# First high halves of the up-projection in one VectorE step, an early split of its third weight chunk, and the last results by TensorE halves and GpSimd

## The chip, the cores and the metric

The kernel runs on one core of one Trainium2 chip. The metric is the device time of one execution in microseconds (us), the median of several runs; lower is better.

## The reference

One layer of a decoder for 256 tokens of width 2048, in float32. Three parts follow one another, each with a norm ahead of it and a norm on its result before the result is added to the residual stream:

```python
x = x + rms_norm(hybrid_mixer(rms_norm(x, mix_pre_norm), ...), mix_post_norm)
h = rms_norm(x, xattn_pre_norm); m = rms_norm(mem, mem_norm)
x = x + rms_norm(cross_attention(h, m, ...), xattn_post_norm)
h = rms_norm(x, ffn_pre_norm)
x = x + rms_norm(conv_glu_ffn(h, w_up, conv_w, conv_b, w_down), ffn_post_norm)
...
def rms_norm(x, g):
    return x * lax.rsqrt(jnp.mean(x * x, axis=-1, keepdims=True) + 1e-6) * g
def conv_glu_ffn(h, w_up, conv_w, conv_b, w_down):
    u = h @ w_up                      # 2048 -> 16384
    uc = conv_b + sum(conv_w[j] * shift_right(u, 2 - j) for j in range(3))
    gate, up = split_cols(uc, (8192, 8192))
    return (jax.nn.gelu(gate, approximate=True) * up) @ w_down   # 8192 -> 2048
```

The change touches two places: the seam between cross-attention and the feed-forward part (the second and third `x = x + ...`), and the last residual addition, which is the output.

## The kernel before

**Three products for one.** Every large matrix product is made in the fast float32r format with compensation. A float32 operand is split into a high half (its rounding to float32r) and a low half (the rest), and TensorE adds up high times high, high times low and low times high. So each weight chunk and each activation tile has a high and a low half: `wh` and `wl` of the weights, and for the up-projection `fh` and `fl` of the normed residual (`hi` and `lo` in the code of `Residual`). ScalarE makes `wh` (L376), VectorE subtracts and gets `wl` (L397).

**Blocks and chunks.** The work is a list of blocks of 256 or 512 output columns, run in a fixed order by `run`. A block's weights come in chunks of 128x1024 (512 KB), each good for two of the 16 contraction tiles k of the up-projection. `Feed` loads the chunks in order through SP's DMA queue into four `raw` buffers; a buffer is free again when its `wl` has been made. `wh` and `wl` have four buffers each too. `feed.hi(n)` and `feed.lo(n)` split all chunks up to number n that are not split yet, in order; `ns` and `nl` count how far that is. The first two blocks of the up-projection (`entry`) are interleaved chunk by chunk, since the tiles of the activation come slowly at first: block 0 chunk 0, block 1 chunk 0, block 0 chunk 1 and so on. With four groups of columns, two tiles and three products, a chunk is 24 matmuls.

**Engines.** Program order on each engine is the order in which the Python code issues. Work beside the matmuls (evacuations, statistics, residuals) is written as generators, of which `run` takes a piece at each `side.half()`, by a budget of VectorE and ScalarE time.

**The seam.** The last block of the output projection of cross-attention (`xo3`) is computed bank by bank, so that the sum of squares for the norm of its result is nearly done when its last columns come. `y_last` has the three parts of that: `after` (once the first bank is done), `mid`, and `gen` at the end. TensorE sums the squares over the partitions (`stb`) and ScalarE makes 1/rms out of it in two steps, `st_b` (called `rb` in `Residual`). `Residual.run` then updates the residual x (`xr`) with the scaled result (`z`): for the first pair of tiles, tile by tile, `z *= rb` and `x += z` on VectorE, then `parts(0)`: `fh = x * g` on ScalarE (float32r) and `fl = x * g - fh` on VectorE, where g is the norm's gain (`pcol("fg", j)`). The factor of the norm itself is applied later, on the products. Later pairs are done two tiles at a time. Only from `fh` of tile 0 on can TensorE begin with the up-projection; until then it runs a few matmuls of no use (`warm`). For the first tile, the order is four times `fh` with `wh`, four times `fh` with `wl`, four times `fl` with `wh`; from the second tile on, `fh` with `wh`, `fl` with `wh`, `fh` with `wl` for each group of columns.

**The end.** `fd_evac` finishes the down-projection: for each half of the tokens (t) and four column groups c of 512, `out = x + z3 * rco`, where `z3` is the product times the gain and `rco` the 1/rms column. For t = 0 all of it runs beside the last matmuls. For t = 1 (`result(1, c)`) it can't. There column group 0 is made by TensorE (identity times x, then a diagonal matrix of `rco` times `z3`, added in PSUM as `sum`) and copied out by ScalarE, which also issues its DMA; groups 1 to 3 are made by VectorE one after the other, and SP issues their DMAs in order.

Of the kernel before, what the change touches and what calls it, by code (L numbers as in the profile page):

```python
# [11 lines left out]
AF = mybir.ActivationFunctionType  # L12
ALU = mybir.AluOpType
AX = mybir.AxisListType

P = 128
D = 2048
S = 256
# [127 lines left out]
def _layer(ctx, tc, nc, d, dbg):  # L146
    act, dve = Meter(nc.scalar, 200.0, 0.83), Meter(nc.vector, 70.0, 1.04)
# [11 lines left out]
    def T2(name, shape=None, dt=F32):  # L159
        return mp.tile(shape or [P, 2, S], dt, tag="T2", bufs=6, name=name)  # L160
# [16 lines left out]
    def aux(name, shape=None):  # L177
        return pp.tile(shape or [P, 512], F32, tag="aux", bufs=4, name=name)

    def mm(out, lhsT, rhs, start=True, stop=True):  # L180
        pe.matmul(out, lhsT, rhs, start=start, stop=stop, skip_group_check=True)  # L181
# [15 lines left out]
    def pcol(n, i=0, w=1):  # L197
        return par[:, PC[n] + i:PC[n] + i + w]
# [131 lines left out]
    class Feed:  # L330
# [49 lines left out]
        def first(self):  # L380
# [8 lines left out]
            self.st[0] = [wh, wl]  # L389
            self.ns = self.nl = 1  # L390

        def lo(self, upto):
            self.hi(upto)
            while self.nl <= min(upto, len(self.src) - 1):
                r = self.raw.pop(self.nl)
                wl = self.staged("wl", r, self.nl)
                nc.vector.tensor_sub(wl, r, self.st[self.nl][0])  # L397
                self.st[self.nl][1] = wl
                self.nl += 1
# [33 lines left out]
    def run():  # L433
# [8 lines left out]
        for b, c0, c1 in order:  # L442
# [23 lines left out]
            for ci, s in enumerate(srcs):  # L466
                if b["pre"]:
                    b["pre"](ci, feed)
                feed.lo(i + 1)
                side.half()  # L470
                side.more = lambda: feed.hi(i + 2)
                ahead = b["xs"](k)
                feed.lo(i + 3)
                feed.dma(i + 6)
                wh, wl = feed.st.pop(i)
                for kj in range(s.shape[1]):
                    xh, xl = b["xs"](k) if kj else ahead
                    first, last = k == 0, k == nk - 1
                    if b["kind"] == "fm":
                        steps = []  # L480
                        for m in range(nm):
                            o = banks[m // 2][:, m % 2]
                            a, c = wh[:, kj, m * P:(m + 1) * P], wl[:, kj, m * P:(m + 1) * P]
                            steps.append([(o, a, xh, first and m % 2 == 0, False), (o, c, xh, False, last),
                                          (o, a, xl, False, False)])
                        if first and entry and b is entry[0]:
                            steps = [[v[0] for v in steps], [v[1] for v in steps], [v[2] for v in steps]]
                        elif b is blocks[0] and k < 4:
                            steps = [[v[0] for v in steps], [v[2] for v in steps], [v[1] for v in steps]]
                        else:  # L490
                            steps = [[v[0], v[2], v[1]] for v in steps]
                        for v in steps:
                            for w in v:
                                mm(*w)
                    elif b is xv:
                        for g in range(2):
                            halves(banks, (wh[:, kj], wl[:, kj], xh, xl), first, last, g)
                    else:
                        for g, o in enumerate(banks):
                            n = o.shape[1]  # L500
                            tm_products(o, g * P * n // b["cols"], g * n % b["cols"], (wh[:, kj], wl[:, kj], xh, xl),
                                        first, last)
                            if len(banks) == 4 and g == 1:
                                side.half()
                    k += 1
                    if kj + 1 < s.shape[1]:
                        side.half()
                i += 1
# [868 lines left out]
    def y_last(b, st, key, gname):  # L1377
        def carry(src, m):
            act.activation(M[key][b // 2][:, (b % 2) * 4 + m], src, AF.Copy, scale=pcol(gname, b * 4 + m))

        def after(ps):
            st.add(ps[0])
            st.fold()

        def mid(ps):
            M["sql"] = C("sql", "bg0", [P, 2, S])
            act.activation(M["sql"][:, 0], ps[1][:, 0], AF.Square)
            for j in range(2):
                carry(ps[0][:, j], j)
            st.ones_of((st.acc[:, 0], M["sql"][:, 0]), start=True)  # L1390

        def gen(ps):
            end = xo3["apart"]
            act.activation(M["sql"][:, 1], end, AF.Square)
            st.ones_of((M["sql"][:, 1],), stop=True)
            carry(ps[1][:, 0], 2)
            st.last()
            yield
            carry(end, 3)
            yield  # L1400
        return after, mid, gen
# [4 lines left out]
    class Residual:  # L1406
# [8 lines left out]
        def run(self):  # L1415
            st, key, hi, lo, gname = self.a
            z, xr = M[key], M["xr"]
            for _ in range(10):
                if st.done:
                    break  # L1420
                yield
            while not st.done:
                side._piece(side.bulk[0])
            if self.early:
                rb = st.row()
            else:
                rb = st.rb
                keep_warm(5)

            def parts(i, js=(0, 1)):  # L1430
                for j in js:
                    k = i * 2 + j
                    act.activation(hi[:, k], part(xr, i)[:, j], AF.Identity, scale=pcol(gname, k))
                for j in js:
                    k = i * 2 + j
                    dve.scalar_tensor_tensor(lo[:, k], part(xr, i)[:, j], pcol(gname, k), hi[:, k],
                                             op0=ALU.mult, op1=ALU.subtract)
                self.ready = i + 1

            def scale(i):  # L1440
                dve.tensor_mul(part(z, i), part(z, i), bc(rb, 2))

            def add(i):
                dve.tensor_add(part(xr, i), part(xr, i), part(z, i))

            if self.early:
                yield
            a, x = part(z, 0), part(xr, 0)
            for j in range(2):
                dve.tensor_mul(a[:, j], a[:, j], rb)  # L1450
                dve.tensor_add(x[:, j], x[:, j], a[:, j])
            if self.early:
                scale(1)
                parts(0)
            else:
                parts(0)
                scale(1)
            yield
            for i in range(1, 8):
                if i == 1:  # L1460
                    add(1)
                if i < 7:
                    scale(i + 1)
                    add(i + 1)
                parts(i)
                if i == 1 and not self.early:
                    side.more()
                if self.early:
                    self.st2.add(part(xr, i - 1))
                    if i == 7:  # L1470
                        self.st2.add(part(xr, 7))
                        self.stats = side.add(self.st2.early_column(), chain=1, free=True)
                elif i == 6:
                    self.stats = side.add(self.squares(), chain=1)
                yield
# [332 lines left out]
    def load_gain():  # L1808
        M["gain"] = mp.tile([P, D], F32, tag="hT", bufs=2, name="gain")
        sp.dma_start(M["gain"], d["fpg"].partition_broadcast(P))  # L1810

    def fd_evac(n):

        def gen(ps):
# [28 lines left out]
            def result(t, c):  # L1843
                f = slice(c % 2 * 512, c % 2 * 512 + 512)
                x, z_ = M["xt"][c // 2][:, t, f], M["z3", c // 2][:, t, f]
                if t and c == 0:
                    diag = C("diag", "ysb0", [P, P])
                    act.activation(diag, ident, AF.Copy, scale=rco[:, t:t + 1])
                    mm(M["sum"], diag, z_, start=False)
                    act.copy(x, M["sum"])  # L1850
                else:
                    dve.scalar_tensor_tensor(x, z_, rco[:, t:t + 1], x, op0=ALU.mult, op1=ALU.add)
                (act if t and c == 0 else sp).dma_start(d["out"][t, :, c * 512:c * 512 + 512], x)
# [17 lines left out]
            result(0, 2)  # L1871
            result(0, 3)
            before_last(1)
            M["sum"] = aux("sum")
            mm(M["sum"], ident, M["xt"][0][:, 1, 0:512], stop=False)
            squares(3)
            finish(1)
            gain(3)
# [101 lines left out]
```

## Time and profile before

| | |
|---|---|
| time, median of 3 runs | 1876.56 us (1876.15 to 1876.88) |
| the profiled execution | 1877.65 us, its span 1875.6 us |
| TensorE (PE) busy | 1865.9 us, 99% of the span |
| VectorE (DVE) busy | 1293.7 us, 69% |
| ScalarE (ACT) busy | 1014.1 us, 54% |
| GpSimd (POOL) busy | 22.3 us, 1% |
| granted TensorE clock | 0.999 of full speed |

The span is what the profiler saw of the device's work; the time of the same execution is 2.05 us longer, and 1.09 us over the median. Times inside the span are counted from its start. In a row of the timeline the first number is the start, the second the duration (of all instructions of the row, if several were merged, "x2"), then engine, line, operation, output<-inputs and shape, and in brackets the idle time of the engine ahead of it with what ended it. In a row of the chain of waits there are start, duration, engine, tile and line. Instructions of one engine overlap a little at their ends, so the next may start before the last has ended. L66 and L181 are helpers through which most instructions go.

### The profile page before, as it was taken

How to read it: one execution, taken by the hardware profiler on the slowest of the kernel's cores; microseconds unless marked ns; L12 is line 12 of the kernel's file. 1: busy time of each engine (PE TensorE's matmuls, PEld its weight loads, DVE VectorE, ACT ScalarE, POOL GpSimd, SP SyncE). 2: the span in 40 equal slices, each digit the busy share in tenths (PEclk: the TensorE clock that was granted, in tenths of full speed). 3: DMA queues.
4: the chain of work that ended last, by engine and by line, in shares of the span. 5: the costliest groups of instructions: out<-in, count | busy, mean ns of one | idle time of the engine just before them, and what ended most of it. 6: DMA issues, size and time to landing. Idle time of an engine off the chain costs nothing.

```text
span 1875.6 us, 36356 instructions
## 1 busy us (share of the span) xinstructions
PE 1865.9 (99%) x15024; PEld 1777.8 (95%) x15024; DVE 1293.7 (69%) x1832; ACT 1014.1 (54%) x1477; POOL 22.3 (1%) x40
## 2 busy tenths in 40 slices
PE   9999999999999999999999999999999999999998
PEld 9999988999999999999999999999999988888887
DVE  7789787566675857687766666777666675566555
ACT  6776445555454645665554445554444555445554
POOL 0000000000000000000000000000000000000000
PEclk9999999999999999999999999999999999999999
DMA  7545544344455765455666666666666666666664
GB/s 266 184 166 195 180 150 161 129 148 157 169 181 204 279 201 183 143 182 167 202 190 192 196 198 192 194 190 192 200 195 194 196 192 215 193 192 196 193 191 145
DMA packets 98197, 351.46 MB, mean 187 GB/s; under 512 B 11056, under 2 KB 11568, under 8 KB 97648
## 3 DMA queue, kind: packets, MB, share of 16 engines
q1 hardware_dynamic: 97168, 348.01, 57.9%
q8 instruction: 117, 1.92, 0.4%
q10 hardware_dynamic: 864, 1.15, 0.2%
q14 instruction: 48, 0.39, 0.1%
HBM read 347.01 MB, written 2.10 MB: 186 GB/s over the span
## 4 chain that ended last, share of the span: by engine, by line
PE 97%; DVE 1%; ACT 1%; DMA 0%; issue 0%; ACTq 0%; DVEq 0%
PE fm L181 67%; PE tm L181 25%; DVE wl L397 1%; PE gram L181 0%; ACT wh L376 0%; PE Y L181 0%; PE lv L181 0%; PE num L181 0%; DMA w<-in_w_in_dram 0%; DVE rows L66 0%; PE X L181 0%; PE gramA L181 0%; PE U L181 0%; PE zg L181 0%; PE zwa L181 0%
## 5 line engine op out<-in xcount | busy, mean ns | idle before, releaser
L397 DVE TENSOR_TENSOR wl<-raw,wh 128x1024 fp32r<-128x1024 f32 (+1 forms) x640 | 776.0, 1217 | 418.5 <-ACT wh L376 415.6
L376 ACT CAST wh<-raw 128x1024 fp32r<-128x1024 f32 (+1 forms) x640 | 664.5, 1043 | 499.9 <-PE fm L181 373.2
L181 PE MATMUL fm<-fh,wh 128*128 128x256 f32 x2048 | 566.4, 277 | 1.4 <-ACT fh L66 1.4
L181 PE MATMUL fm<-fh,wl 128*128 128x256 f32 x2048 | 565.5, 276 | 0.0
L181 PE MATMUL fm<-fl,wh 128*128 128x256 f32 x2048 | 565.4, 276 | 0.0
L181 PEld LDWEIGHTS fm<-fh,wh 128*128 128x128 f32 x2048 | 384.3, 188 | 1.5 <-ACT fh L66 1.5
L181 PEld LDWEIGHTS fm<-fh,wl 128*128 128x128 f32 x2048 | 384.7, 188 | 0.1
L181 PEld LDWEIGHTS fm<-fl,wh 128*128 128x128 f32 x2048 | 384.3, 188 | 0.0
L181 PE MATMUL tm<-wh,as 128*128 128x512 f32 x1024 | 315.3, 389 | 0.0
L181 PE MATMUL fm<-hh,wh 128*128 128x256 f32 x1024 | 285.2, 281 | 0.2
L181 PE MATMUL fm<-hh,wl 128*128 128x256 f32 x1024 | 282.4, 278 | 0.7 <-DVE wl L397 0.7
L181 PE MATMUL fm<-hl,wh 128*128 128x256 f32 x1024 | 282.2, 278 | 0.0
L181 PEld LDWEIGHTS tm<-wh,as 128*128 128x128 f32 x1024 | 192.1, 188 | 40.0
L181 PE MATMUL tm<-wl,as 128*128 128x512 f32 x512 | 199.2, 389 | 0.0
L181 PEld LDWEIGHTS fm<-hh,wh 128*128 128x128 f32 x1024 | 192.4, 189 | 1.8 <-issue 0.3
L181 PEld LDWEIGHTS fm<-hh,wl 128*128 128x128 f32 x1024 | 191.4, 188 | 1.1 <-DVE wl L397 1.1
L181 PEld LDWEIGHTS fm<-hl,wh 128*128 128x128 f32 x1024 | 191.9, 188 | 0.1
L181 PEld LDWEIGHTS tm<-wl,as 128*128 128x128 f32 x512 | 96.1, 188 | 19.9
L66 ACT CAST as<-ac 128x256 fp32r<-128x256 f32 x128 | 45.6, 404 | 110.8 <-PE tm L181 110.8
L66 DVE TENSOR_TENSOR as<-ac,as 128x256 fp32r<-128x256 f32 x128 | 48.5, 421 | 61.7 <-ACT as L66 61.7
L181 PE MATMUL fm<-mgh,wh 128*128 128x256 f32 x256 | 71.0, 277 | 0.0
L181 PE MATMUL fm<-mgh,wl 128*128 128x256 f32 x256 | 70.8, 277 | 0.0
(383 smaller groups left out, 2220.3 us busy)
## 6 DMA issues: line engine op xcount, KB each, us to landing
raw<-in_w_fu_dram SPq DMA_DIRECT2D x256, 512.0 KB, 4.2
raw<-in_w_in_dram SPq DMA_DIRECT2D x152, 512.0 KB, 3.6
raw<-in_w_fd_dram SPq DMA_DIRECT2D x128, 512.0 KB, 3.9
raw<-in_w_br_dram SPq DMA_DIRECT2D x32, 512.0 KB, 3.8
raw<-in_w_mo_dram SPq DMA_DIRECT2D x32, 512.0 KB, 3.9
raw<-in_w_xk_dram SPq DMA_DIRECT2D x8, 512.0 KB, 4.1
raw<-in_w_xv_dram SPq DMA_DIRECT2D x8, 512.0 KB, 3.8
raw<-in_w_xq_dram SPq DMA_DIRECT2D x8, 512.0 KB, 3.6
```

The lines of the kernel that those rows point to most:

```text
L66: return f(out, *a, **k)
L181: pe.matmul(out, lhsT, rhs, start=start, stop=stop, skip_group_check=True)
L376: nc.scalar.copy(wh, r)
L397: nc.vector.tensor_sub(wl, r, self.st[self.nl][0])
```

## The change

The change has three parts.

**The seam.** `y_last.after` now also makes `xg = x * g` for tiles 0 and 1 on ScalarE, before the norm's factor is known. When `rb` is there, the high half comes from one VectorE instruction, `fh = z * g + xg` (`head`), which doesn't wait for `x += z`; that addition moves to GpSimd. `fl = x * g - fh` (`rest`) stays on VectorE and waits for GpSimd.

**The third weight chunk.** `feed.early` splits chunk number 2 of the up-projection (both halves) on VectorE, ahead of the seam's own VectorE work; before, ScalarE and VectorE did it after the first two pairs of tiles.

**The end.** The PSUM tile `sum` becomes two of 128x256, copied out one after the other by ScalarE. Of column group 1, VectorE makes only the first 256 columns, and GpSimd makes the other 256 in two instructions.

```diff
+        def early(self, i):
+            r = self.raw.pop(i)
+            wh, wl = self.staged("wh", r, i), self.staged("wl", r, i)
+            nc.vector.tensor_copy(wh, r)
+            nc.vector.tensor_sub(wl, r, wh)
+            self.st[i] = [wh, wl]
+            self.ns, self.nl = i + 1, i + 1
...
                 feed.lo(i + 1)
+                if entry and b is entry[0] and ci == 0 and c0 == 0:
+                    feed.early(i + 2)
                 side.half()
...
         def after(ps):
             st.add(ps[0])
             st.fold()
+            M["xg"] = T2("xg")
+            for j in range(2):
+                act.activation(M["xg"][:, j], M["xr"][0][:, j], AF.Identity, scale=pcol("fg", j))
...
             a, x = part(z, 0), part(xr, 0)
-            for j in range(2):
-                dve.tensor_mul(a[:, j], a[:, j], rb)
-                dve.tensor_add(x[:, j], x[:, j], a[:, j])
             if self.early:
+                for j in range(2):
+                    dve.tensor_mul(a[:, j], a[:, j], rb)
+                    dve.tensor_add(x[:, j], x[:, j], a[:, j])
                 scale(1)
                 parts(0)
             else:
-                parts(0)
+                def head(j):
+                    dve.scalar_tensor_tensor(hi[:, j], a[:, j], pcol(gname, j), M["xg"][:, j], op0=ALU.mult, op1=ALU.add)
+
+                def rest(j):
+                    dve.scalar_tensor_tensor(lo[:, j], x[:, j], pcol(gname, j), hi[:, j], op0=ALU.mult, op1=ALU.subtract)
+
+                for j in range(2):
+                    dve.tensor_mul(a[:, j], a[:, j], rb)
+                    pool.tensor_tensor(x[:, j], x[:, j], a[:, j], op=ALU.add)
+                    if j == 0:
+                        head(0)
+                rest(0)
+                head(1)
+                rest(1)
+                self.ready = 1
                 scale(1)
...
+    E4 = [slice(0, S), slice(S, 2 * S)]
...
                 if t and c == 0:
                     diag = C("diag", "ysb0", [P, P])
                     act.activation(diag, ident, AF.Copy, scale=rco[:, t:t + 1])
-                    mm(M["sum"], diag, z_, start=False)
-                    act.copy(x, M["sum"])
+                    for q, v in zip(M["sum"], E4):
+                        mm(q, diag, z_[:, v], start=False)
+                    for q, v in zip(M["sum"], E4):
+                        act.copy(x[:, v], q)
+                elif t and c == 1:
+                    v = E4[1]
+                    pool.tensor_scalar(z_[:, v], z_[:, v], rco[:, t:t + 1], None, op0=ALU.mult)
+                    pool.tensor_tensor(x[:, v], x[:, v], z_[:, v], op=ALU.add)
+                    v = E4[0]
+                    dve.scalar_tensor_tensor(x[:, v], z_[:, v], rco[:, t:t + 1], x[:, v], op0=ALU.mult, op1=ALU.add)
                 else:
                     dve.scalar_tensor_tensor(x, z_, rco[:, t:t + 1], x, op0=ALU.mult, op1=ALU.add)
...
-            M["sum"] = aux("sum")
-            mm(M["sum"], ident, M["xt"][0][:, 1, 0:512], stop=False)
+            M["sum"] = [aux("sum", [P, S]) for _ in E4]
+            for q, v in zip(M["sum"], E4):
+                mm(q, ident, M["xt"][0][:, 1, v], stop=False)
```

How this stands in the engines' queues. First VectorE at the seam, from the folding of the last sum of squares (`st`) on; before:

```order
L66 TENSOR_TENSOR st_9647<-st_9647 128x256
L397 TENSOR_TENSOR wl<-raw,wh 128x1024
L66 TENSOR_TENSOR z_9645<-z_9645,st_b 128x256
L66 TENSOR_TENSOR xr_7859<-xr_7859,z_9645 128x256
L66 TENSOR_TENSOR z_9645<-z_9645,st_b 128x256
L66 TENSOR_TENSOR xr_7859<-xr_7859,z_9645 128x256
L66 SCALAR_TENSOR_TENSOR fl<-xr_7859,par,fh 128x256 x2
L66 TENSOR_TENSOR z_9645<-z_9645,st_b 128x512
```

and after the change:

```order
L406 TENSOR_TENSOR wl<-raw,wh 128x1024
L396 CAST wh<-raw 128x1024
L397 TENSOR_TENSOR wl<-raw,wh 128x1024
L66 TENSOR_TENSOR z_9645<-z_9645,st_b 128x256
L66 SCALAR_TENSOR_TENSOR fh<-z_9645,par,xg 128x256
L66 TENSOR_TENSOR z_9645<-z_9645,st_b 128x256
L66 SCALAR_TENSOR_TENSOR fl<-xr_7859,par,fh 128x256
L66 SCALAR_TENSOR_TENSOR fh<-z_9645,par,xg 128x256
L66 SCALAR_TENSOR_TENSOR fl<-xr_7859,par,fh 128x256
L66 TENSOR_TENSOR z_9645<-z_9645,st_b 128x512
```

The two instructions of the third chunk (L396, L397) come in front of the first `z`, the two additions to `xr` are gone, and two that make `fh` have come. (L397 of before is L406 of after.)

Then ScalarE, from the last full square (`sq`) of the first bank to the first tiles' `fh`; before:

```order
L66 ACTIVATE sq<-fm 128x512
L376 CAST wh<-raw 128x1024
L66 ACTIVATE sql<-fm 128x256
L66 ACTIVATE z_9646<-fm,par 128x256 x2
L1694 DMA cv<-in_conv_dram 128x512
L66 ACTIVATE sql<-fm 128x256
L66 ACTIVATE z_9646<-fm,par 128x256
L66 ACTIVATE st_b<-stb,mhalf 128x256
L66 ACTIVATE st_b<-st_b 128x256
L66 ACTIVATE z_9646<-fm,par 128x256
L66 ACTIVATE fh<-xr_7859,par 128x256 x4
L376 CAST wh<-raw 128x1024 x3
```

and after the change, from behind the same `sq` on:

```order
L66 ACTIVATE xg<-xr_7859,par 128x256 x2
L376 CAST wh<-raw 128x1024
L66 ACTIVATE sql<-fm 128x256
L66 ACTIVATE z_9646<-fm,par 128x256 x2
L1722 DMA cv<-in_conv_dram 128x512
L66 ACTIVATE sql<-fm 128x256
L66 ACTIVATE z_9646<-fm,par 128x256
L66 ACTIVATE st_b<-stb,mhalf 128x256
L66 ACTIVATE st_b<-st_b 128x256
L66 ACTIVATE z_9646<-fm,par 128x256
L66 ACTIVATE fh<-xr_7859,par 128x256 x2
L376 CAST wh<-raw 128x1024 x2
```

The two `xg` stand ahead of a weight cast and of the squares of the last bank (`sql`); two `fh` and one weight cast are gone behind `st_b`.

Last, GpSimd's queue to its end (the `_c` tiles are 1/rms columns); before:

```order
L226 TENSOR_TENSOR stm_c<-var,mhalf 128x2
L226 TENSOR_TENSOR sty_c<-var,mhalf 128x2
L226 TENSOR_TENSOR stx_c<-var,mhalf 128x2
L226 TENSOR_TENSOR stf_c<-var,mhalf 128x2
L1976 UNCONDITIONAL_BRANCH
```

and after the change:

```order
L226 TENSOR_TENSOR stx_c<-var,mhalf 128x2
L1478 TENSOR_TENSOR xr_7859<-xr_7859,z_9645 128x256 x2
L226 TENSOR_TENSOR stf_c<-var,mhalf 128x2
L1885 TENSOR_SCALAR z_19872<-z_19872,rco 128x256
L1886 TENSOR_TENSOR xt<-xt,z_19872 128x256
```

Four instructions have come, two at the seam and two at the end. On TensorE only the four matmuls of 128x256 stand in place of two of 128x512 for `sum`; SP's order is unchanged.

## The prediction

> **What bounds the kernel now.** I read the page first: busy times, and the chain that ended last.
>
> ```profile
> PE 1865.9 (99%) x15024; PEld 1777.8 (95%) x15024; DVE 1293.7 (69%) x1832; ACT 1014.1 (54%) x1477; POOL 22.3 (1%) x40
> PE 97%; DVE 1%; ACT 1%; DMA 0%; issue 0%; ACTq 0%; DVEq 0%
> ```
>
> TensorE is the bound: 97% of the chain is its own work. What can be won is the few stretches in which it waits, or the rate of its matmuls. The change touches two such waits. The first shows in the chain in order of time, from 811 to 870 us:
>
> ```profile
> 813.19 0.39 ACT sql L66
> ...
> 813.63 0.71 PE stb L181 x2
> ...
> 814.36 0.48 ACT st_b L66
> ...
> 814.87 0.42 ACT st_b L66
> ...
> 815.32 0.44 DVE z L66
> ...
> 815.77 0.44 DVE xr L66
> ...
> 816.24 0.52 ACT fh L66
> ...
> 816.79 45.51 PE fm L181 x384
> ```
>
> From 813.2 to 816.8 us all hangs on one string: last squares, their sum, 1/rms, z, x, fh, first matmul. From the start of z to the first matmul it is 816.79 - 815.32 = 1.47 us.
>
> Then TensorE's rate, from its timeline around the third weight chunk and the chain further on:
>
> ```profile
> 822.47 0.28 PE L181 MATMUL fm<-fl,wh 128*128 128x256 f32 x1
> 822.70 0.38 PE L181 MATMUL fm<-fh,wl 128*128 128x256 f32 x1
> ...
> 831.99 0.28 PE L181 MATMUL fm<-fh,wl 128*128 128x256 f32 x1
> ```
>
> ```profile
> 869.29 10.90 PE fm L181 x96
> ...
> 937.32 10.91 PE fm L181 x96
> 948.66 571.22 PE fm L181 x5040
> ```
>
> Matmuls of one shape run at two rates. From 869.29 on each takes 10.90/96 = 0.1135 us. Between the rows at 822.70 and 831.99 lie 78 steps; without the wait of 0.11 (0.23 us from 822.47 to 822.70, where 0.113 is usual; it shows again in the next step) each takes 0.1177 us. Ahead of 822.47 the rate is the fast one: 49 steps from 816.79 take 5.68 us, 0.13 of it start-up. So the short wait at the third chunk is followed by some 46 us at the slow rate, up to the first transposes of x just ahead of 869.29. Why there are two rates no row says.
>
> **The change part by part.** VectorE's, ScalarE's and one TensorE row of the seam:
>
> ```profile
> 811.13 1.22 DVE L397 TENSOR_TENSOR wl<-raw,wh 128x1024 fp32r<-128x1024 f32 x1
> 815.32 0.42 DVE L66 TENSOR_TENSOR z<-z,st_b 128x256 f32<-128x256 f32 x1 [2.97 <-ACT st_b L66]
> ...
> 817.57 0.48 DVE L66 SCALAR_TENSOR_TENSOR fl<-xr,par,fh 128x256 fp32r<-128x256 f32 x1 [0.18 <-ACT fh L66]
> ...
> 821.42 1.22 DVE L397 TENSOR_TENSOR wl<-raw,wh 128x1024 fp32r<-128x1024 f32 x1
> ```
>
> ```profile
> 809.92 1.04 ACT L376 CAST wh<-raw 128x1024 fp32r<-128x1024 f32 x1
> ...
> 810.86 0.39 ACT L66 ACTIVATE sql<-fm 128x256 f32<-128x256 f32 x1
> 811.14 0.84 ACT L66 ACTIVATE z<-fm,par 128x256 f32<-128x256 f32 x2
> ```
>
> ```profile
> 811.86 0.59 PE L181 MATMUL stb<-sql,ones 128*128 128x256 f32 x2
> ```
>
> A. *xg.* Two ScalarE instructions like the two of z at 811.14 (0.84 us) now stand ahead of the weight cast and of sql. ScalarE has no idle time there, so sql ends at 810.86 + 0.39 + 0.84 = 812.09 instead of 811.25. TensorE takes it up at 811.86; behind it in its queue are the last six products of the bank, whose squares start the string at 813.19. They move by 812.12 - 811.86 = 0.26 us. Bounds: 0 if the last squares were bound by something else, 0.84 if nothing covered. I take +0.26; ScalarE's idle time ahead of the second sql covers the rest.
>
> B. *fh in one step.* After z (0.45 to the next dependent start) comes one VectorE instruction of the kind at 817.57 (0.48); with the 0.04 from fh to TensorE that is 0.97 in place of 1.47: -0.50.
>
> C. *What is late next.* TensorE now wants fl of tile 0 after eight matmuls, at 0.97 + 8 x 0.1133 = 1.88 us from z, then fh of tile 1 four matmuls later, and its fl one more later. VectorE makes in order z0, fh0, z1, fl0, fh1, fl1, and each fl waits for GpSimd's addition. Nothing of 128x256 elements with two inputs runs on GpSimd before. The nearest rows, and what GpSimd does beside VectorE:
>
> ```profile
> L216 POOL CAST bones<-bf 128x128 fp32r<-128x128 f32 x1 | 0.3, 290 | 0.1
> ```
>
> ```profile
> 71.96 0.23 POOL L744 COPY rows<-rows 4x64 f32<-4x64 f32 x1 [1.86 <-DVE rows L66]
> 72.90 1.56 POOL L744 COPY rows<-rows 4x64 f32<-4x64 f32 x2 [0.71 <-DVE rows L66]
> 718.78 1.70 POOL L226 TENSOR_TENSOR sty_c<-var,mhalf 128x2 f32<-128x2 f32 x1 [52.80 <-DVE var L66]
> 764.91 0.70 POOL L226 TENSOR_TENSOR stx_c<-var,mhalf 128x2 f32<-128x2 f32 x1 [44.43 <-DVE var L66]
> ```
>
> ```profile
> 72.77 1.21 DVE L397 TENSOR_TENSOR wl<-raw,wh 128x1024 fp32r<-128x1024 f32 x1
> 73.90 0.86 DVE L66 SCALAR_TENSOR_TENSOR rr<-pr,par,rr 128x255 f32<-128x255 f32 x2
> 718.70 1.22 DVE L397 TENSOR_TENSOR wl<-raw,wh 128x1024 fp32r<-128x1024 f32 x1
> ```
>
> A cast of 128 columns takes 0.29 us. Twice the columns and two inputs give at most four times that, 1.16; I take the middle of the logarithm, about 0.65. The other rows show exclusion: the same 128x2 instruction takes 0.70 us alone and 1.70 us when a TENSOR_TENSOR of two SBUF inputs (718.70 to 719.92) runs, and the copies at 72.90 stand still until wl ends at 73.98. But then both are done by 74.46, beside the SCALAR_TENSOR_TENSORs of 73.90 to 74.76, which themselves take their usual 0.86. So I take it that z excludes GpSimd and fh, fl don't. With that, z1 and the first addition go one after the other (0.85 to about 1.6), fl0 is ready at 2.1, fh1 at 2.5, fl1 at 3.0; TensorE waits 0.2 and then 0.35: +0.55. With no exclusion at all it is +0.16 (fl1 at 2.58 where 2.45 is wanted). With exclusion by every instruction of two SBUF inputs, GpSimd gets in only when VectorE stands: additions from 1.27 to 2.57, fl0 at 3.05, fl1 at 3.95: +1.49.
>
> The Trainium skill's "SBUF — State Buffer", section on the two separate sides, states that last case: GpSimd and VectorE share a port pair as an exclusive lock, held for the whole instruction, and a VectorE instruction with two SBUF inputs takes it against a GpSimd one that reads SBUF. The row at 718.78 agrees, the one at 72.90 doesn't; by the page the sum below would be 2.0 us higher.
>
> D. *Third chunk early.* The cast is at most twice this one of 128x512:
>
> ```profile
> 4.79 0.43 DVE L383 CAST wh<-w 128x512 fp32r<-128x512 f32 x1 [4.79 <-DMA w<-in_w_in_dram]
> ```
>
> so 0.86 + 1.22 = 2.08 us, in VectorE's idle 2.97, which A changes to 2.97 - 0.84 + 0.26 = 2.39. It fits; without that cover the 2.08 would stand in the string. The wl at 821.42 goes, and with it the wait at 822.47: -0.12. Its fl of tiles 2 and 3 precede that row and were done in time. The raw buffer comes free earlier, so SP issues the next load some 7 us sooner, with nothing queued behind it that waits.
>
> E. *The rate.* With no wait at the third chunk, TensorE can keep the fast rate to 862.30 (the end of the 384): 384 - 50 = 334 steps x (0.1177 - 0.1135) = 1.4, and the two pieces of 24 behind it 0.2 more, which the interruptions by the statistic may spoil. Ends 0 and -1.6. C's waits could start the slow rate as the wait at 822.47 did, but they are longer, and the start at 816.79 after over a microsecond of waiting gave the fast one. I take -1.5.
>
> F. *The end.*
>
> ```profile
> 1869.17 0.21 ACT rco L66
> ...
> 1869.87 1.14 PE sum L181 x2
> ...
> 1871.03 0.59 ACT xt L66
> ```
>
> ```profile
> 1869.46 2.07 DVE L66 SCALAR_TENSOR_TENSOR xt<-z,rco,xt 128x512 f32<-128x512 f32 x3
> ```
>
> ```profile
> 1871.64 0.36 ACTq L1853 DMA_DIRECT2D out_dram<-xt  x1
> ```
>
> ```profile
> out_dram<-xt SPq DMA_DIRECT2D x7, 256.0 KB, 2.4
> out_dram<-xt ACTq DMA_DIRECT2D x1, 256.0 KB, 3.0
> ```
>
> ScalarE's DMA lands last (1871.64 + 3.0; VectorE's results end at 1871.53). Its copy now ends a half copy (0.39, as sql) after the matmuls instead of 0.59: -0.20. VectorE has half an instruction less, about 0.28. GpSimd has 0.48 and 0.65 from 1869.45 on, to 1870.6 if SCALAR_TENSOR_TENSORs leave it alone; SP's DMA of column group 1 waits for that, and those of groups 2 and 3 are queued behind it. If they shut it out, GpSimd begins at 1871.25, ends at 1872.4, SP issues its third DMA at about 1873.1, and that lands at 1875.5 instead of 1874.6: +0.9. I take -0.2.
>
> Sum: 0.26 - 0.50 + 0.55 - 0.12 - 1.5 - 0.2 = -1.5 us on the span of 1875.6; the 2.05 us around it stay, so the profiled execution's 1877.65 would be 1876.1. That execution is 1.09 above the median, so the median of 1876.56 becomes 1875.0.
>
> **The rivals.** *The slow rate stays* (C's waits start it): A to D and F alone, 0.0, with some slow steps more: 1876.6. For it: the 0.11 wait at 822.47 did just that. Against: the start at 816.79.
>
> *Every pair of SBUF inputs shuts GpSimd out* (C at 1.49, F at +0.9): 0.26 - 0.50 + 1.49 - 0.12 + 0.9 = +2.0, so 1878.6, or 1877.1 if the fast rate comes: slower than before. It decides from about 0.6 us of extra waiting at the two places together if the fast rate doesn't come.
>
> *The slow rate holds through the up-projection*: if the transposes of x no longer end it, 7 x 96 + 5040 = 5712 steps x 0.0043 = +24 us, 1900. Against it: all seven stretches after transposes are fast, the first of them out of the slow rate.
>
> *The early split does nothing* because VectorE's idle time no longer holds it (A later than worked out): the string grows by up to 0.8: inside the range.
>
> **How the numbers follow.** Forecast 0.47, slow rate stays 0.29, exclusion throughout 0.15, slow rate to the end 0.04, none of these 0.05. The forecast's own range is 1873.9 (A at 0, C at 0.16, E at -1.6, with 0.35 for the spread of runs) to 1875.9. To leave out no more than 2 in 10 it reaches from 1873.8 over the second case to 1877.8, into the third. About 0.2%, 3.75 us, is what a measurement of this kernel tells from no change: faster than 1872.8 asks for more than all gains at their ends, 0.03; slower than 1880.3 is the fourth case and a little of the third, 0.06; within 0.91.
>
> **What would show it.** A: sql ends near 812.1. B: first matmul 0.97 after z. C: GpSimd's additions of 0.65, TensorE's waits for fl 0.2 and 0.35. D: wl of the third chunk before 815.6 and no wait at it. E: 0.1135 per matmul up to 862. F: ScalarE's last copy ends near 1871.4 on the old clock, less the shift. It is wrong if GpSimd takes over 1 us for an addition, or the rate is slow behind 869.

## Result, and the profile after

| | before | after |
|---|---|---|
| time, median of 17 runs each | 1876.80 us (1876.12 to 1878.83) | 1879.82 us (1878.62 to 1881.08) |
| ratio | | 1.0016 (95%: 1.0009 to 1.0023) |
| the profiled execution, its span | 1877.65 us, 1875.6 us | 1879.36 us, 1877.6 us |

The changed kernel is 3.0 us (0.16%) slower; the forecast was 1.6 us faster, in a range that ended at 1877.8. The difference is inside the 3.75 us that the prediction called no change, but the interval of the ratio is 1.7 to 4.3 us: a small loss, clear of the spread, where a small gain was forecast. Of the 11 executions of the changed kernel in experiment 10 one took 3306.88 us at a granted clock of 0.685; it is left out there, which makes their median 1878.93 us instead of 1879.37.

The program ahead of the seam is unchanged, so the shift of 0.76 us with which this profile comes to the seam (it is there by 43 us) is not the change's; a second profile of before comes there 1.2 us later than the first. All steps below are therefore counted from an event just ahead of them.

**The seam.** ScalarE's, VectorE's and GpSimd's timelines after the change, and the two TensorE rows that begin with a wait (in brackets, with what ended it):

```profile
810.19 0.60 ACT L66 ACTIVATE sq<-fm 128x512 f32<-128x512 f32 x1 [0.85 <-PE fm L181]
810.69 0.90 ACT L66 ACTIVATE xg<-xr,par 128x256 f32<-128x256 f32 x2
...
814.29 0.39 ACT L66 ACTIVATE sql<-fm 128x256 f32<-128x256 f32 x1 [0.76 <-PE fm L181]
```

```profile
814.48 1.22 DVE L397 TENSOR_TENSOR wl<-raw,wh 128x1024 fp32r<-128x1024 f32 x1
816.42 0.42 DVE L66 TENSOR_TENSOR z<-z,st_b 128x256 f32<-128x256 f32 x1 [0.71 <-ACT st_b L66]
816.88 0.48 DVE L66 SCALAR_TENSOR_TENSOR fh<-z,par,xg 128x256 fp32r<-128x256 f32 x1
817.28 0.96 DVE L66 TENSOR_TENSOR z<-z,st_b 128x256 f32<-128x256 f32 x1
818.16 0.47 DVE L66 SCALAR_TENSOR_TENSOR fl<-xr,par,fh 128x256 fp32r<-128x256 f32 x1
818.56 0.95 DVE L66 SCALAR_TENSOR_TENSOR fh<-z,par,xg 128x256 fp32r<-128x256 f32 x1
819.61 0.49 DVE L66 SCALAR_TENSOR_TENSOR fl<-xr,par,fh 128x256 fp32r<-128x256 f32 x1
```

```profile
816.98 0.98 POOL L1478 TENSOR_TENSOR xr<-xr,z 128x256 f32<-128x256 f32 x1 [50.61 <-PE warm L181]
818.38 0.84 POOL L1478 TENSOR_TENSOR xr<-xr,z 128x256 f32<-128x256 f32 x1 [0.43 <-DVE z L66]
```

```profile
817.42 0.74 PE L181 MATMUL fm<-fh,wh 128*128 128x256 f32 x4 [0.88 <-DVE fh L66]
...
820.16 0.39 PE L181 MATMUL fm<-fl,wh 128*128 128x256 f32 x1 [0.21 <-DVE fl L66]
```

Look at the durations of like instructions on VectorE. z of tile 0 takes 0.42 us, z of tile 1 0.96; fh of tile 0 takes 0.48, fh of tile 1 0.95. The two long ones are those that start while an addition of GpSimd runs, and they end 0.28 and 0.29 us after it has ended (817.96 and 818.24; 819.22 and 819.51). So here VectorE lost 0.54 and 0.47 us to GpSimd. The first product comes 1.00 us after z, as foreseen, but fl of tile 1 is ready only at 820.10, 3.68 us after z.

**The end.** VectorE's, GpSimd's and SP's rows after the change:

```profile
1869.56 1.94 DVE L66 SCALAR_TENSOR_TENSOR xt<-z,rco,xt 128x256 f32<-128x256 f32 x3
```

```profile
1869.58 1.17 POOL L1885 TENSOR_SCALAR z<-z,rco 128x256 f32<-128x256 f32 x1 [1005.76 <-ACT rco L66]
1870.83 1.24 POOL L1886 TENSOR_TENSOR xt<-xt,z 128x256 f32<-128x256 f32 x1
```

```profile
1872.10 0.33 SPq L1891 DMA_DIRECT2D out_dram<-xt  x1
...
1872.53 0.40 SPq L1891 DMA_DIRECT2D out_dram<-xt  x1
...
1873.02 0.41 SPq L1891 DMA_DIRECT2D out_dram<-xt  x1
```

VectorE is done at 1871.50. GpSimd ends at 1872.07, and only then does SP issue the DMA of group 1 and, queued behind it, those of groups 2 and 3, which were ready by 1871.50. SP's last issue stands 3.51 us after ScalarE began `diag` (1869.51); before, it was 1871.55 - 1869.41 = 2.14 us. SP's issues to the output before the change (first and last start behind the comma):

```profile
L1853 SPq DMA_DIRECT2D out_dram<-xt x5: 332/332/333, 1867.5 to 1871.5; - x5
```

### The profile page after: what moved, and what is told of

Same layout as the page of the kernel before. It is cut to its first block, busy times and chain, and to the rows that moved or that the text cites. A ratio compares the mean times of both kernels' runs of the same rounds, so it can differ in the third digit from the quotient of the medians.

```text
span 1877.6 us, 36378 instructions
## 1 busy us (share of the span) xinstructions
PE 1865.5 (99%) x15028; PEld 1777.2 (95%) x15028; DVE 1295.4 (69%) x1833; ACT 1013.4 (54%) x1477; POOL 26.5 (1%) x44
## 4 chain that ended last, share of the span: by engine, by line
PE 87%; issue 9%; DVE 2%; ACT 1%; DMA 0%; POOLq 0%; ACTq 0%; DVEq 0%; POOL 0%
PE fm L181 67%; PE tm L181 16%; DVE wl L406 1%; ACT wh L376 0%; PE gram L181 0%; PE Y L181 0%; PE lv L181 0%; PE num L181 0%; DMA w<-in_w_in_dram 0%; DVE rows L66 0%; PE X L181 0%; PE gramA L181 0%; PE U L181 0%; PE zg L181 0%; PE zwa L181 0%
## 5 line engine op out<-in xcount | busy, mean ns | idle before, releaser
L406 DVE TENSOR_TENSOR wl<-raw,wh 128x1024 fp32r<-128x1024 f32 (+1 forms) x639 | 774.9, 1217 | 419.3 <-ACT wh L376 416.5
```

## Experiments

All edits are against the kernel before unless said otherwise. In this table, worked out from the timelines, "sq to sql" is the time from the start of ScalarE's last 512-column squares ahead of the seam (810.19 in the rows above) to that of its last 256-column squares; then come the times from z to the first product, from z to the 25th matmul (the second chunk), and for the 12 matmuls from the 49th to the 61st (the third chunk). "All" goes from sq to the 61st matmul. "Rate" is that of the 320 matmuls from there on, in us each.

| kernel | sq to sql | z to first | z to 25th | 49th to 61st | all | rate |
|---|---|---|---|---|---|---|
| before | 3.76 | 1.47 | 4.32 | 1.62 | 14.55 | 0.1178 |
| before, again | 3.77 | 1.48 | 4.33 | 1.59 | 14.53 | 0.1133 |
| end alone | 3.78 | 1.48 | 4.31 | 1.61 | 14.54 | 0.1133 |
| halves alone | 3.77 | 1.48 | 4.32 | 1.61 | 14.55 | 0.1133 |
| end, DMA last | 3.77 | 1.48 | 4.31 | 1.61 | 14.53 | 0.1133 |
| before, with the series of experiment 5 behind it | 3.76 | 1.48 | 4.41 | 1.41 | 14.54 | 0.1133 |
| early chunk alone | 3.76 | 1.48 | 4.41 | 1.41 | 14.54 | 0.1178 |
| after | 4.10 | 1.00 | 5.11 | 1.36 | 15.42 | 0.1133 |
| after, again | 4.10 | 1.00 | 5.10 | 1.36 | 15.41 | 0.1133 |
| after without the end | 4.09 | 1.00 | 5.13 | 1.41 | 15.59 | 0.1178 |
| ... and xg later | 3.76 | 1.00 | 5.11 | 1.36 | 15.08 | 0.1133 |
| ... additions on VectorE | 4.10 | 1.00 | 4.94 | 1.36 | 15.24 | 0.1133 |
| ... xg later, operands in PSUM | 3.77 | 1.00 | 4.34 | 1.36 | 14.28 | 0.1133 |

At one rate these stretches repeat within 0.03 us from profile to profile, whereas single executions of one kernel differ by up to 4 us. So the terms are read here, and the medians only bound their sum.

**1. The end alone.** The two parts of the diff in `fd_evac`, nothing else.

> The kernel before with the change at the end alone: PSUM halves for column group 0, GpSimd for half of column group 1. Theory (GpSimd takes about 1.2 us for each of its two 128x256 instructions, and SP's two last DMAs are queued behind the one that waits for it): 1.9 to 2.2 us slower than before, with the third DMA of SP issued about 1.9 us later after diag. Rival (the end costs at most the 0.9 us that the prediction gave as its bound, the rest of the loss comes from the seam): 0 to +0.9 us.

Measured: 1878.31 us, against 1876.69 before: ratio 1.0007 (0.9999 to 1.0016). GpSimd's two rows took 1.17 and 1.25 us, SP's last issue came 3.5 us after `diag`, and the span ended 7.62 us after it, against 6.20 (both by the trace's unrounded times): +1.42. In the two profiles of the full change it was 8.06 both times, +1.86. The theory's mechanism holds and the profile passes the rival's +0.9, but 1.9 to 2.2 was too much. The further 0.44, with every issue at the same place, lies behind the last landing. SP waits there for its DMAs and then for TensorE's queue (PEq; total us, times, longest); the last wait is longer after the full change than before, or than with the end alone (0.6 too). After, then before:

```profile
SPq L2015 <- DMA out_dram<-xt: 2.6, 1, 2.6
SPq L2015 <- PEq L2015: 1.1, 2, 0.9
```

```profile
SPq L1976 <- PEq L1976: 0.6, 2, 0.4
```

Why it is longer stays open.

**2. Seam and early chunk, without the end.**

> The changed kernel without its change at the end: seam and early third chunk alone. Theory: seam about +1.2 us (xg +0.3, fh in one step -0.5, GpSimd's additions +1.3), early chunk and kept fast rate -1.8 us, together 0.4 to 0.8 us faster than before. Rival (the seam's waits start the slow rate in most executions, and the profiled one was lucky): 0.8 to 1.5 us slower than before.

Measured: 1878.18 against 1876.69, ratio 1.0007 (0.9998 to 1.0015). The theory's number is wrong; the rival's is met. The seam's terms came again (table: +0.33 up to sql, -0.47 up to the first product, 0.81 more than before up to the 25th matmul). But the matmuls ran at the slow rate although no wait at the third chunk was left. That the seam's waits start that rate, the rival's reason, doesn't fit the full change, which has the same waits and ran fast in two profiles.

**3. The early chunk alone.**

```diff
+        def early(self, i):
...
                 feed.lo(i + 1)
+                if entry and b is entry[0] and ci == 0 and c0 == 0:
+                    feed.early(i + 2)
```

> The kernel before with the early split of the third weight chunk alone. Theory (the wait at that chunk starts 46 us at the slow matmul rate): the matmuls from the first of the up-projection to 862 us take 0.1135 us each, 1.5 to 1.8 us faster than before. Rival (the rate has its own reasons): only the wait itself goes, 0.1 to 0.2 us faster.

Measured: 1877.60 against 1876.69, ratio 1.0002 (0.9994 to 1.0011). The theory falls. The rival's gain can't be read either: the wait is gone (1.41 instead of 1.62 in the table), but here the steps ahead of it ran at the slow rate too. The chain of this kernel shows the 384 matmuls of the first two blocks as slow as they were before:

```profile
817.43 45.50 PE fm L181 x384
```

and the chain of the kernel with the end alone, whose code up to there is that of before, wait included, shows them fast:

```profile
817.55 44.04 PE fm L181 x384
```

**4. TensorE halves without GpSimd.** `sum` in two halves of 256 columns, each copied by itself; VectorE makes all of group 1.

> The kernel before with column group 0 of the last results added and copied by PSUM halves, and no GpSimd. Theory: ScalarE's last DMA is issued 0.2 us sooner, so 0.2 us faster, or less where SP's last DMA (issued at 1871.5) then ends the span. Rival (two half copies cost more than one whole): 0 to +0.2 us.

Measured: 1876.93 against 1876.69, ratio 1.0002 (0.9993 to 1.0011). ScalarE's DMA is issued 2.03 us after `diag` instead of 2.23, as expected, but the span ends 6.19 us after it instead of 6.20. SP's last issue stands where it stood (2.14 us), and so it is now the later of the two. The last column has the time from issue to landing, in us:

```profile
out_dram<-xt ACTq DMA_DIRECT2D x1, 256.0 KB, 2.8
out_dram<-xt SPq DMA_DIRECT2D x1, 256.0 KB, 3.0
```

Before, SP's last DMA took 2.5 and ScalarE's 3.0. So the last landing was ScalarE's, 2.23 + 3.0 = 5.2 us after `diag`, and is now SP's, at 2.14 + 3.0 = 5.1: the end of the span stays.

**5. GpSimd by itself.** Behind the last DMA a series on scratch tiles u, v (VectorE) and a, b (GpSimd), each 128x256, each piece begun by a one-column VectorE instruction, such as

```diff
+    for _ in range(6):
+        V.scalar_tensor_tensor(v, u, r1, v, op0=ALU.mult, op1=ALU.add)
+    for _ in range(2):
+        G.tensor_tensor(a, a, b, op=ALU.add)
```

> The kernel before with a series of scratch instructions behind its last DMA (the output is that of before; the time is longer by the series and is not compared). GpSimd's additions and multiplications of 128x256 fp32 alone, then additions of 64 and 128 columns, then pairs of them beside six VectorE instructions: TENSOR_TENSOR, SCALAR_TENSOR_TENSOR (twice, the second time beside GpSimd's multiplication), a copy of one input, SCALAR_TENSOR_TENSOR with one input in PSUM, and beside ScalarE copies. Theory (exclusion by any VectorE instruction with two SBUF inputs): alone an addition takes 0.55 to 0.7 us; beside TENSOR_TENSOR and SCALAR_TENSOR_TENSOR either it or VectorE stands still for the other's whole time, so the two engines together take the sum of their times; beside PSUM inputs and ScalarE both run at their own speed. Rival 1 (only TENSOR_TENSOR excludes, the reading of the prediction): beside SCALAR_TENSOR_TENSOR both keep their own time. Rival 2 (no exclusion; GpSimd simply takes 0.85 to 1.25 us): alone 0.85 or more.

GpSimd's timeline: alone (the first four rows), then two beside six of VectorE's TENSOR_TENSOR, SCALAR_TENSOR_TENSOR (twice), COPY and SCALAR_TENSOR_TENSOR with one input in PSUM:

```profile
1873.87 2.32 POOL L1903 TENSOR_TENSOR pa<-pa,pb 128x256 f32<-128x256 f32 x3 [1010.51 <-DVE pb L1899]
1876.57 2.96 POOL L1906 TENSOR_SCALAR pb<-pb,ones 128x256 f32<-128x256 f32 x3 [0.38 <-DVE pb L1899]
1879.81 1.11 POOL L1910 TENSOR_TENSOR pa<-pa,pb 128x64 f32<-128x64 f32 x3 [0.28 <-DVE pa L1908]
1881.19 1.52 POOL L1910 TENSOR_TENSOR pa<-pa,pb 128x128 f32<-128x128 f32 x3 [0.27 <-DVE pa L1908]
1882.98 1.82 POOL L1915 TENSOR_TENSOR pa<-pa,pb 128x256 f32<-128x256 f32 x2 [0.27 <-DVE pb L1899]
1886.81 1.58 POOL L1920 TENSOR_TENSOR pa<-pa,pb 128x256 f32<-128x256 f32 x2 [2.00 <-DVE pb L1899]
1891.12 2.35 POOL L1925 TENSOR_SCALAR pb<-pb,ones 128x256 f32<-128x256 f32 x2 [2.73 <-DVE pb L1899]
1894.68 1.62 POOL L1930 TENSOR_TENSOR pa<-pa,pb 128x256 f32<-128x256 f32 x2 [1.22 <-DVE pb L1926]
1897.78 1.52 POOL L1935 TENSOR_TENSOR pa<-pa,pb 128x256 f32<-128x256 f32 x2 [1.48 <-DVE pb L1899]
```

and VectorE's beside them:

```profile
1882.93 3.53 DVE L1913 TENSOR_TENSOR db<-db,da 128x256 f32<-128x256 f32 x6
...
1886.76 3.99 DVE L1918 SCALAR_TENSOR_TENSOR db<-da,ones,db 128x256 f32<-128x256 f32 x6
...
1891.05 3.28 DVE L1923 SCALAR_TENSOR_TENSOR db<-da,ones,db 128x256 f32<-128x256 f32 x6
...
1894.63 2.81 DVE L1928 COPY db<-da 128x256 f32<-128x256 f32 x6
...
1897.74 3.08 DVE L1933 SCALAR_TENSOR_TENSOR db<-pq,ones,db 128x256 f32<-128x256 f32 x6
```

A row of several includes the gaps between them, 0.08 us from one addition to the next. By itself an addition alone takes 0.72 us and a multiplication 0.92; the theory had 0.55 to 0.7 for the addition. Six SCALAR_TENSOR_TENSORs take 3.08 us with one input in PSUM and 3.99 with both in SBUF: there the two that run beside GpSimd's additions take 1.05 and 0.83 us, the other four 0.49 each. So two additions cost VectorE 0.91 us, while they themselves take 0.72 and 0.78. Where VectorE comes first, GpSimd pays too: its first addition beside TENSOR_TENSOR takes 0.96. Beside GpSimd's multiplication, which reads one tensor, VectorE loses only 0.20 in all, and GpSimd's two take 1.21 and 1.04. So rival 1, the prediction's reading, is out, and so is rival 2. The theory is right that SCALAR_TENSOR_TENSOR excludes too and that PSUM inputs and ScalarE don't (0.72 per addition beside both); the sum of both times was too much. And it misses the copy, which has one SBUF input: two of the six take 0.69 and 0.77 us, the other four 0.29.

**6. xg later.** As 2, with the two instructions of `xg` moved behind the copies of z in `mid`.

> Seam and early chunk without the end, as in the run without the end, but ScalarE makes xg behind the squares and the two copies of z, in its idle 0.76 us. Theory (A costs the string what xg pushes the last squares by): the string from the fold of the sums to z is shorter by 0.3 to 0.4 us than with xg ahead of the squares. Rival (the last squares wait for TensorE in any case): no change, or later by up to 0.1 where 0.84 us of xg do not fit the idle time.

Measured: sq to sql 3.76 us as before, the whole stretch 15.08 instead of 15.42: -0.34. The theory holds. By the clock 1878.60 against 1877.22, ratio 1.0007 (0.9998 to 1.0016), which can't resolve this.

**7. The additions on VectorE.** As 2, without GpSimd:

```diff
-                    pool.tensor_tensor(x[:, j], x[:, j], a[:, j], op=ALU.add)
...
+                    head(j)
+                    dve.tensor_add(x[:, j], x[:, j], a[:, j])
+                    rest(j)
```

> Seam and early chunk without the end, with the two additions of x on VectorE, in the order z, fh, x, fl for each tile. Theory (GpSimd's additions hold VectorE up by 0.54 and 0.47 us, as much as VectorE would need for them): fl of tile 1 ends 3.6 to 3.8 us from the start of z, as with GpSimd, and TensorE's 60 steps behind the first product take as long within 0.15 us. Rival (GpSimd's additions are hidden beside VectorE's work): 0.5 to 0.9 us longer.

```profile
815.62 0.43 DVE L66 TENSOR_TENSOR z<-z,st_b 128x256 f32<-128x256 f32 x1 [0.70 <-ACT st_b L66]
...
818.65 0.48 DVE L66 SCALAR_TENSOR_TENSOR fl<-xr,par,fh 128x256 fp32r<-128x256 f32 x1
```

fl of tile 1 ends 819.13 - 815.62 = 3.51 us after z, with GpSimd 3.68; the stretch is 15.24 against 15.42. Both are a little quicker than the theory's figures, and the rival is out. Giving the additions to GpSimd was worth less than nothing. Timed: 1877.86 against 1877.22, ratio 1.0002 (0.9994 to 1.0011).

**8. The DMA of group 1 last.** As 1, with `sp.dma_start` of group 1 behind those of groups 2 and 3.

> The kernel before with the change at the end alone, but the DMA of column group 1 queued behind those of groups 2 and 3. Theory (of the 1.4 to 1.9 us that the end costs, 0.9 are the two DMA issues queued behind the one that waits for GpSimd): SP's last issue comes 0.7 to 0.9 us sooner after diag than with the DMA in order, and the median is 0.6 to 1.2 us over before. Rival (the landing of the DMAs sets the end, not their issue): as with the DMA in order, 1.4 to 1.9 us over before.

```profile
1869.14 0.99 SPq L1864 DMA_DIRECT2D out_dram<-xt  x2
1870.38 0.33 SPq L1893 DMA_DIRECT2D out_dram<-xt  x1
```

With `diag` at 1867.79, SP's last issue comes after 2.59 us instead of 3.51, and the span ends 6.82 us after `diag` instead of 7.62, still 0.62 later than before the change. In the profile the theory holds; the last landing, too, comes sooner (2.59 + 3.2 = 5.8 us after `diag` instead of 3.51 + 3.0 = 6.5). The theory's 0.6 to 1.2 us over before is not met by the median, 1876.77 against 1877.22 (ratio 1.0000, 0.9991 to 1.0009), whose interval reaches from -1.7 to +1.7 us.

**9. One SBUF input.** As 6, with 1/rms (`rb`) and `xg` in PSUM:

```diff
-            act.activation(self.rb, self.rb, AF.Exp, scale=-0.5)
+            act.activation(self.q, self.rb, AF.Exp, scale=-0.5)
+            self.rb = self.q
...
-            M["xg"] = T2("xg")
+            M["xg"] = aux("xg", [P, 2, S])
```

> As the run with xg behind the squares (seam and early chunk, no change at the end), but 1/rms and xg lie in PSUM, so that z and fh have one SBUF input each; fl and GpSimd's additions keep two. Theory (the hold is between instructions with two SBUF inputs and GpSimd): z of tile 1 takes 0.42 us instead of 0.95, fh of tile 1 0.48 instead of 0.95; fl of tile 1 ends 2.9 to 3.2 us from the start of z instead of 3.68, TensorE's 24 steps start 0.4 to 0.7 us sooner, and the stretch from the last squares ahead of the seam to the 60th step is 14.3 to 14.7 us, level with before (14.55). Rival (GpSimd's reads hold VectorE up whatever its other input): 0.95 each and 15.1 us as without PSUM.

```profile
816.79 0.41 DVE L66 TENSOR_TENSOR z<-z,stb 128x256 f32<-128x256 f32 x1
817.25 0.48 DVE L66 SCALAR_TENSOR_TENSOR fl<-xr,par,fh 128x256 fp32r<-128x256 f32 x1
817.65 0.47 DVE L66 SCALAR_TENSOR_TENSOR fh<-z,par,xg 128x256 fp32r<-128x256 f32 x1
818.36 0.48 DVE L66 SCALAR_TENSOR_TENSOR fl<-xr,par,fh 128x256 fp32r<-128x256 f32 x1 [0.24 <-POOL xr L1479]
```

z and fh of tile 1 take 0.41 and 0.47 us instead of 0.96 and 0.95, although GpSimd is adding (1.84 us for the two, from 816.49). The theory holds: what held VectorE in z and fh was their second SBUF input. The stretch is 14.28 us, 0.27 under before. That is also what the early chunk alone gives once its slow rate is taken out (60 x 0.0044 = 0.26 of its 14.54), so the seam's new order gains nothing even then. Timed: 1877.18 against 1876.45, ratio 1.0003 (0.9994 to 1.0012): no kernel here beats the one before by anything that can be measured.

**10. Both kernels again.**

> The changed kernel itself once more, for a second profile and a comparison on the chip of the other runs. Theory (the matmul rate from 824 us on is chance, seam and end are not): stretch of the seam 15.4 us or 15.5 at the slow rate, end 7.6 to 8.1 us from diag, while the rate behind the seam and in the first 100 us may be either; 2 to 3 us slower than before. Rival (the rate follows the early chunk): fast up to 862 us as in the first profile.

> The kernel before once more, for a second profile. Theory (chance): seam 14.55 us again, and the rate behind the third chunk fast or slow alike. Rival (the wait at the third chunk starts the slow rate): slow from about 824 us on, 46 us long, as in its first profile.

After: 1878.93 against 1876.45, ratio 1.0015 (1.0006 to 1.0024), seam and end as in its first profile. Before, one execution of 1877.27: the chain shows the same 384 matmuls, wait at the third chunk included, at the fast rate:

```profile
817.99 44.04 PE fm L181 x384
```

So the rival is out: with the wait the rate behind it was slow in one profile of five, without it in two of seven. The profile of experiment 5, again the code of before, has the prediction's order reversed: its matmuls ran at 0.1178 us from the first product up to the third chunk, so that almost nothing was left of the wait, and at 0.1133 behind it.

## Why the prediction was wrong

| step | predicted | measured | from |
|---|---|---|---|
| A, xg ahead of sql | +0.26 | +0.34 | sq to sql, 4.10 - 3.76 |
| B, fh in one step | -0.50 | -0.47 | z to first product |
| C, waits for fl | +0.55 | +1.26 | z to 25th, 5.11 - 4.32, less B |
| D, wait at the third chunk | -0.12 | -0.25 | 49th to 61st, 1.36 - 1.61 |
| E, the rate | -1.5 | 0: no link with the wait | rate column |
| F, the end | -0.2 | +1.4 to +1.9 | from `diag` to the span's end |
| sum | -1.5 | +2.3 to +2.7 | measured medians: +3.0 and +2.5 |

**E failed as a step.** The prediction took one profile's order of events, a wait and then 46 us at the slow rate, for cause and effect. The same code ran fast there in five further profiles, and two kernels without the wait ran slow. So the expected gain of 1.5 us belonged to the one execution shown, not to the code. Its own evidence against, that the far longer wait ahead of the first product left the rate fast, was in the text and was overruled.

**F failed as a step, in three places.** GpSimd's two instructions were put at 0.48 and 0.65 us; alone they take 0.92 and 0.72 (experiment 5), which is 0.51 more. Beside VectorE's SCALAR_TENSOR_TENSORs, which the prediction took to leave GpSimd alone, they took 1.17 and 1.24, 0.77 more again; an addition of over 1 us was the prediction's own sign of being wrong. So SP's last issue, queued behind the DMA that waits for them, came 1.37 us later.

The third place is the landings, taken as fixed: 2.4 us for SP's DMAs, 3.0 for ScalarE's. ScalarE's does land last before the change, as the prediction read it. But the 3.0 belongs to the DMA that is issued last and close behind another, not to ScalarE: in experiment 4 SP's last DMA takes it, and ScalarE's saving of 0.20 moves nothing. With the end alone SP's last DMA lands 3.51 + 3.0 = 6.5 us after `diag`, 1.3 later than ScalarE's did before. That is the cost of 1.4, since the span ends 1.0 to 1.1 us behind the last landing in both, and in experiments 4 and 8. The bound of +0.9 had SP's last issue at about the right place (1873.1), but gave it 2.4 us to land.

**C was mis-sized, because its exclusion was misread.** The copies at 72.90, on which "fh and fl don't exclude GpSimd" rested, read one tensor of 4x64; the additions read two of 128x256. Experiment 5 shows that such a row couldn't stand for the additions: VectorE's SCALAR_TENSOR_TENSORs lose 0.91 us beside two additions, 0.20 beside two multiplications, which read one tensor. Whether the number of tensors makes the difference was not tested by itself. The measured 1.26 is near the bound of 1.49. The Trainium skill's page "SBUF — State Buffer", section on the two separate sides, which the prediction gave less weight than that row, was right in the main: a lock between GpSimd and a VectorE instruction with two SBUF inputs, taken by whoever starts first. Experiment 9 agrees (0.41 and 0.47 us with one input moved to PSUM). That the other waits for the whole instruction is more than was measured: two additions of 0.72 and 0.78 us cost VectorE 0.91. Nor did the one that started first always win: the SCALAR_TENSOR_TENSOR that started at 1886.76 in experiment 5, ahead of the addition at 1886.81, was one of the two held up (1.05).

**A, B and D were right** in mechanism: xg delayed the last squares through TensorE's queue (undone in experiment 6), the first product came 1.00 us after z, and the split of the third chunk fitted VectorE's gap (ended 815.70, z at 816.42). D was twice its forecast, since the step behind the wait was long too (0.22 us, as the wait's own step); the prediction had seen that and counted one.

Of the rivals, "every pair of SBUF inputs shuts GpSimd out" had the mechanism and the sign. At 1878.6 it was 1.2 us low; its term F was 0.9 where 1.4 to 1.9 were measured.

## What to carry to other kernels

GpSimd is no free second VectorE: price its instruction by itself first, and then, if VectorE's instruction beside it has two SBUF inputs or copies from SBUF to SBUF, count more than half of the overlap as lost. A DMA that waits for the slowest producer belongs last in its queue. Read the end of the span from the last landing, and expect the DMA issued last to take longer. Before a rate seen once in a trace is put into a sum, look for a second profile of the same code, and if there is none give it no more than an even chance.

## What the runs showed of the hardware

- GpSimd, fp32, 128 partitions, alone: additions of 64, 128 and 256 columns 0.32, 0.45 and 0.72 us, with 0.08 between two; a multiplication by a per-partition scalar of 256 columns 0.92 us, slower than the addition although it reads one tensor less.
- Two GpSimd additions beside VectorE instructions with two SBUF inputs cost VectorE 0.9 us, beside copies from SBUF to SBUF as much (0.69 and 0.77 us instead of 0.29); beside SCALAR_TENSOR_TENSORs with one input in PSUM nothing that shows (3.08 us for six, 0.72 per addition).
- Matmuls of one shape ran at 0.1133 or 0.1178 us over some 40 us at the same place of the same code, in different executions, at a granted clock of 0.999 or 1.0 (mean over the span, experiment 5 with its idle end aside). What sets it was not found.
- The span ended 1.0 to 1.1 us after the last DMA of 256 KB had landed, and 1.5 in the two profiles of the full change. DMAs to the output that SP issued 0.66 us apart landed after 2.4 us, the last one, issued 0.1 to 0.6 behind another, after 3.0 to 3.2.
